# A DiT layer in float32: DeltaNet heads cut into five pieces among the next heads' projections, query latents ahead of the latents of keys and values

## The chip, the cores and the metric

The kernel runs on one core of one Trainium2 chip. The metric is the device time of one execution in microseconds (us). In the profile PE is the tensor engine's matmuls and PEld its weight loads, DVE the vector engine, ACT the scalar engine, POOL the GpSimd engine and SP the engine whose queue issues all DMAs. Each engine works through its own queue in the order in which the program left it, and waits there for the results that an operation needs.

## The reference

One layer of a hybrid diffusion backbone: 256 latent tokens and 256 context tokens of width 2048, all float32. Cut to what matters here:

```
h = modulate(rmsnorm(x), shift, scale)              # latent and context tokens
q_a, kv_a, k_rope, dq, dk, dv, dz, gates... = split(h @ w_in)
# latent attention (8 heads)
k, v = mla_kv(kv_a, k_rope, ...)                    # rmsnorm(kv_a) @ w_kv_b, head norm, rotary
q    = mla_q(q_a, ...)                              # rmsnorm(q_a) @ w_q_b, head norm, rotary
y_mla = attend_latent(q, k, v, context keys and values)
# gated DeltaNet (8 heads, chunks of 64, two directions)
k = l2norm(silu(conv3(dk))); v = silu(conv3(dv)); q = l2norm(silu(conv3(dq))) * 128**-0.5
m   = strict_lower(beta * (k k^T) * decay)          # one 64 x 64 matrix per chunk, head, direction
sol = triangular_solve(I + m, rhs)                  # the kernel inverts I + m
scan over the chunks with sol, k * decay, q * decay, (q k^T) * decay
# then gates, output projections, and a gated MLP with a depthwise convolution
```

## The kernel before

A float32 product is made of two or three products of rounded parts: a weight tile is loaded in halves of 128 x 1024 (`raw`, four buffers), and each 512 columns are split by ACT (`whi`, the rounded copy) and DVE (`wlo`, the rest), six buffers of each. `mm_hl` then issues a pair of matmuls for each 128 rows of the contraction: `whi` against 512 columns (both parts of the activations), `wlo` against 256. The activations are `H[0]` (latent tokens; `h_92` in the order of instructions) and `H[1]` (context tokens; `h_93`). A projection (`proj`) of 128 output columns runs over 16 such rows for one or both token sets (`segs`), so it takes 16 or 32 pairs.

The part that the change touches comes after the first norm. For each DeltaNet head, `head_inputs` projects keys (`wdk`) and values (`wdv`) for both token sets and queries (`wdq`) for the latent tokens; for the heads 0, 1 and 2 keys and values exist already (`dkx`). `dn_head` then does the head's own work: `dn_unit` is the convolution (DVE, tile `cy`), a tanh on ACT (`ct`), the squares (`sqk`), their column sums on PE (`sp`), the scale (`l2m`: DVE, then a power on POOL), two diagonal tiles (`rb_d`, DVE), which a pair of matmuls spreads over all partitions (`bp`), and the scaled result `KT` or `QT`, with its mirrored copy for the backward direction from ACT. The K products `kk` give `U`, which goes to memory in six DMAs (`Ud`, `Uo`); `qk` gives `A`; the values' tile is `VT`; K and V are turned by eight PE transposes each (`tp`) into `KE` and stored. The heads come in the order 0, 3, 1, 4, 2, 5, 6, 7. Beside all this `ada`, a generator, adds up the rest of the modulation vector on DVE (`acc`, one 128 x 512 tile `rawa` of weights per unit, 256 units in all); here it gets a budget of 4,000 (`ADB`) per head, at 650 a unit.

After the heads, `inverse` loads all `U` (`ux<-Ud`), runs 60 dependent operations on DVE (`ux<-ux`), copies the result (`xt`, ACT) and stores it in 32 small DMAs (`Xd`, `Xs`). It is given `IK` of budget after each of the four projections of the latents of keys and values (`wkva`, tile `kvx`), and `IQ` after each of the four of the query latents (`wqa`, tile `qax`). The norms of both (`bk`, `bq`), the split latents `kvn` and `qan_`, and the rotary key (`krf`, which is copied by a DMA to the other half of the partitions and then split to `krt`) follow. `fill` is a generator of gate projections (tile `gtp`, weights `wz`, then `wgm`), 16 pairs a tile, that is drawn on as filler. The attention then begins with the keys (`kps`), their norm (`ksq`, `ks`) and the values (`vps`), beside the first off-diagonal products of the inversion (`ivp`, with tiles `xd` loaded from `Xd`).

A scheduler takes the program in the order in which it is written as priority, and settles from that and its own model the fixed order of each engine's queue.

Of the kernel before, what the change touches and what calls it, by code (L numbers as in the profile page):

```python
# [25 lines left out]
N1 = 3  # L26
# [15 lines left out]
OD = 8000  # L42
OC = 4000
WO = 900
IK = 5000
IQ = 4000
NW = 3
R0 = 1.3
R1 = 1.0
# [4 lines left out]
@with_exitstack  # L54
def hybrid_block(ctx: ExitStack, tc: tile.TileContext, io, dbg=None):
    nc = tc.nc
    act, dve, pool, pe, sync = nc.scalar, nc.vector, nc.gpsimd, nc.tensor, nc.sync


    def pool_(name, bufs, side="left"):  # L60
# [90 lines left out]

        pool.tensor_tensor(out=out, in0=in_, in1=half.broadcast_to([P, n]), op=ALU.pow)

    def row_bcast(pl, ps, r, n):
# [6 lines left out]
        for k, v in enumerate((rh, rl)):  # L161
            dg = pl.tile([P, n, P], F32R, tag="rb_d", name="rb_d", bufs=2)
            dve.tensor_tensor(out=dg, in0=idb, in1=v.unsqueeze(2).broadcast_to([P, n, P]), op=ALU.mult)
            pe.matmul(ps[:, : n * P], onesr, dg.rearrange("p a b -> p (a b)"), start=k == 0, stop=k == 1)
# [234 lines left out]
    pB = ctx.enter_context(ExitStack())  # L399
    pb = pB.enter_context(pool_("pb", 1))  # L400

    def proj(src, segs):
        W = load_w(src)
        pss = [psm.tile([P, 512], F32, tag="mm", name="mmp") for _ in segs]
        for k in range(KD):
            for ps, s in zip(pss, segs):
                mm_hl(ps, P, W(k * P), H[s][:, k], k == 0, k == KD - 1)
        return pss


# [114 lines left out]
        act.activation(t, y, AF.Tanh)  # L525
        return y, t

    def dn_unit(x, f, ns, post, dst):
# [3 lines left out]
        sq = pb.tile([P, 2, T], F32, tag="ct", name="sqk")[:, :ns]  # L532
        act.activation(sq, y, AF.Square)
        n = 2 * ns
# [5 lines left out]
        dve.tensor_scalar(out=m, in0=sp[:, :n], scalar1=post, scalar2=EPS * post, op0=ALU.mult, op1=ALU.add)  # L540
        rsq(pb, m, m, n)
        bp = psa.tile([P, 512], F32, tag="aux", name="bp")
        row_bcast(pb2, bp, m, n)
        for s in range(ns):
            dve.tensor_tensor(out=dst[:, 4 * s : 4 * s + 4, 0], in0=bp[:, s * T : (s + 1) * T].rearrange("p (s i) -> p s i", i=64),
                              in1=y[:, s].rearrange("p (s i) -> p s i", i=64), op=ALU.mult)
        reverse(dst, ns)
# [4 lines left out]
            act.copy(v[:, :, 1], v[:, ::-1, 0, ::-1])  # L552

    def dn_head(h, kx, vx, qx):
        KT = pb2.tile([P, 8, 2, 64], F32, tag="KT", name="KT")
        dn_unit(kx, 8 + h, 2, 1.0, KT)
        sync.dma_start(KTs[:, :, h].rearrange("s p c -> p s c"), KT.rearrange("p s d i -> p s (d i)"))
        QT = pb2.tile([P, 4, 2, 64], F32, tag="QT", name="QT")
        dn_unit(qx, h, 1, 128.0, QT)
# [21 lines left out]
        y, t = dn_conv(vx, 16 + h, 2)  # L581
        VT = pb2.tile([P, 8, 2, 64], F32, tag="KT", name="VT")
        dve.scalar_tensor_tensor(out=VT[:, :, 0], in0=t.rearrange("p a (s i) -> p (a s) i", i=64), scalar=1.0,
                                 in1=y.rearrange("p a (s i) -> p (a s) i", i=64), op0=ALU.add, op1=ALU.mult)
        reverse(VT, 2)
        for which, src, scr in (("k", KT, KEs), ("v", VT, Vs)):
            o = pb2.tile([P, 8, P], F32, tag="KE", name="KE")
            for q in range(2):
                tp = psa.tile([P, 4, P], F32, tag="aux", name="tp")
                for j in range(4):  # L590
                    pe.transpose(tp[:, j], src[:, 4 * q + j].rearrange("p d i -> p (d i)"), ident)
                if which == "k":
                    dve.tensor_tensor(out=o[:, 4 * q : 4 * q + 4], in0=tp,
                                      in1=kb[:, 4 * q : 4 * q + 4, h].unsqueeze(2).broadcast_to([P, 4, P]), op=ALU.mult)
                else:
                    act.copy(o[:, 4 * q : 4 * q + 4], tp)
            sync.dma_start(scr[:, :, h].rearrange("s p c -> p s c"), o)

    def head_inputs(h):
        if h < N1:  # L600
            xs = [dkx[:, 2 * h], dkx[:, 2 * h + 1]]
        else:
            xs = []
            for w in ("wdk", "wdv"):
                pss = proj(io[w][h], (0, 1))
# [138 lines left out]
    kvx = pn.tile([P, 4, 2, T], F32, name="kvx")
    for f in range(4):
        pss = proj(io["wkva"][f], (0, 1))
        for s in range(2):
            gather(pss[s], P, kvx[:, f, s])
        inv(IK)
    bk = pn.tile([P, 2, T], F32, name="bk")  # L750
    rms_bcast(pn2, 4, lambda k: (kvx[:, k, 0], kvx[:, k, 1]), 1.0 / 512, bk)
    qax = pn.tile([P, 4, T], F32, name="qax")
    for f in range(4):
        gather(proj(io["wqa"][f], (0,))[0], P, qax[:, f])
        if f == 2:
            for k in range(4):
                dve.scalar_tensor_tensor(out=kvx[:, k], in0=kvx[:, k], scalar=kvan[:, k : k + 1], in1=bk, op0=ALU.mult, op1=ALU.mult)
                split(kvx[:, k], kvn[:, k, 0], kvn[:, k, 1])
        inv(IQ)
# [22 lines left out]
    dve.tensor_tensor(out=krf[0:64, 0], in0=krf[0:64, 0], in1=rt[0:64], op=ALU.add)  # L782
    sync.dma_start(krf[64:128], krf[0:64])
# [591 lines left out]
```

## Time and profile before

| | us |
|---|---|
| median of 3 runs | 1940.28 (1939.37 to 1945.17) |
| profiled execution | 1937.21 |
| its span on the core | 1935.4 |
| PE busy | 1826.2 |
| DVE busy | 1437.0 |
| ACT busy | 915.9 |

A row of the profile's groups names line, engine, operation, the tile written and the tiles read, and the count. "Idle before" is the time that the engine stood still just ahead of such an operation, with what ended it. A row of the timeline gives start, duration, and in brackets the wait ahead of it. PE's granted clock is 1.00 at full speed, so that busy time at a lower clock holds less work.

### The profile page before, as it was taken

How to read it: one execution, taken by the hardware profiler on the slowest of the kernel's cores; microseconds unless marked ns; L12 is line 12 of the kernel's file. 1: busy time of each engine (PE TensorE's matmuls, PEld its weight loads, DVE VectorE, ACT ScalarE, POOL GpSimd, SP SyncE). 2: the span in 40 equal slices, each digit the busy share in tenths (PEclk: the TensorE clock that was granted, in tenths of full speed). 3: DMA queues.
4: the chain of work that ended last, by engine and by line, in shares of the span. 5: the costliest groups of instructions: out<-in, count | busy, mean ns of one | idle time of the engine just before them, and what ended most of it. 6: DMA issues, size and time to landing. Idle time of an engine off the chain costs nothing.

```text
span 1935.4 us, 34978 instructions
## 1 busy us (share of the span) xinstructions
PE 1826.2 (94%) x13186; PEld 1552.7 (80%) x13186; DVE 1437.0 (74%) x2854; ACT 915.9 (47%) x1882; POOL 41.7 (2%) x45
## 2 busy tenths in 40 slices
PE   7889988999879999999999997999999999999999
PEld 5677867788678878778888885888888888888887
DVE  4998887777768778656679888887778777755554
ACT  3224443333367656543245545555554555544443
POOL 0000000000000000000000000000000000000000
PEclk7899988999889999999999998999999999999999
DMA  8984576665676777788776886776667565566664
GB/s 319 317 290 163 170 202 204 202 195 183 124 239 209 221 223 227 239 254 260 227 266 206 259 282 201 251 252 184 189 203 236 186 184 186 179 195 200 194 193 128
DMA packets 222521, 418.26 MB, mean 216 GB/s; under 512 B 71504, under 2 KB 113616, under 8 KB 219920
## 3 DMA queue, kind: packets, MB, share of 16 engines
q1 hardware_dynamic: 222352, 416.04, 69.1%
q8 instruction: 103, 1.69, 0.4%
q14 instruction: 66, 0.54, 0.1%
HBM read 387.00 MB, written 28.84 MB: 215 GB/s over the span
## 4 chain that ended last, share of the span: by engine, by line
PE 50%; issue 10%; DMA 6%; DVE 4%; ACT 1%; POOL 0%; SPq 0%; POOLq 0%; DVEq 0%; ACTq 0%
PE fps L141 13%; PE dps L141 8%; PE fps L142 7%; DMA rawa<-in_wada 5%; PE gtp L141 5%; PE dps L142 4%; PE gtp L142 2%; DVE acc L240 1%; DVE wlo L101 1%; PE brp L141 1%; PE kp L1084 1%; PE fps L139 1%; PE yp L1093 1%; DMA raw<-in_wgate 1%; PE op L1105 1%
## 5 line engine op out<-in xcount | busy, mean ns | idle before, releaser
L101 DVE TENSOR_TENSOR wlo<-raw,whi 128x512 fp32r<-128x512 f32 (+1 forms) x940 | 634.9, 685 | 197.4 <-ACT whi L100 186.2
L100 ACT CAST whi<-raw 128x512 fp32r<-128x512 f32 (+1 forms) x940 | 571.7, 618 | 415.5 <-PE dps L141 117.4
L141 PE MATMUL fps<-H,whi 128*128 128x512 f32 x1290 | 461.9, 399 | 5.8 <-DVE H L101 5.8
L142 PE MATMUL fps<-H,wlo 128*128 128x256 f32 x1290 | 363.7, 282 | 2.4 <-DVE wlo L101 2.4
L141 PEld LDWEIGHTS fps<-H,whi 128*128 128x128 f32 x1290 | 243.3, 189 | 62.3 <-DVE H L101 4.8
L142 PEld LDWEIGHTS fps<-H,wlo 128*128 128x128 f32 x1290 | 244.8, 190 | 7.7 <-DVE wlo L101 4.0
L240 DVE SCALAR_TENSOR_TENSOR acc<-rawa,sc,acc 128x512 f32<-128x512 f32 x240 | 179.2, 747 | 76.7 <-DMA rawa<-in_wada 75.4
L141 PE MATMUL mmp<-h,whi 128*128 128x512 f32 x600 | 225.2, 413 | 0.9 <-ACT whi L100 0.9
L141 PE MATMUL gtp<-h,whi 128*128 128x512 f32 x600 | 220.8, 404 | 0.0
L141 PE MATMUL dps<-GB,whi 128*128 128x512 f32 x544 | 193.0, 397 | 0.0
L142 PE MATMUL mmp<-h,wlo 128*128 128x256 f32 x600 | 174.8, 292 | 7.7 <-DVE wlo L101 7.7
L142 PE MATMUL gtp<-h,wlo 128*128 128x256 f32 x600 | 171.0, 285 | 0.0
L142 PE MATMUL dps<-GB,wlo 128*128 128x256 f32 x544 | 153.1, 282 | 0.0
L141 PEld LDWEIGHTS mmp<-h,whi 128*128 128x128 f32 x600 | 117.5, 196 | 27.7 <-ACT whi L100 1.3
L141 PEld LDWEIGHTS gtp<-h,whi 128*128 128x128 f32 x600 | 113.6, 189 | 25.8 <-issue 1.5
L142 PEld LDWEIGHTS mmp<-h,wlo 128*128 128x128 f32 x600 | 118.1, 197 | 10.2 <-DVE wlo L101 8.4
L141 PEld LDWEIGHTS dps<-GB,whi 128*128 128x128 f32 x544 | 102.1, 188 | 25.3
L142 PEld LDWEIGHTS gtp<-h,wlo 128*128 128x128 f32 x600 | 114.2, 190 | 4.2 <-issue 1.0
L142 PEld LDWEIGHTS dps<-GB,wlo 128*128 128x128 f32 x544 | 102.5, 188 | 0.0
L344 PE MATMUL fp<-h,gh 128*128 128x256 f32 (+1 forms) x224 | 60.9, 306 | 17.0 <-ACT h L335 17.0
L319 DVE CUSTOM_DVE_ANT_0 junk<-wt,scb 128x2048 bf16<-128x2048 f32 x32 | 73.1, 2284 | 0.1
L345 PE MATMUL fp<-h,gh 128*128 128x256 f32 (+1 forms) x224 | 65.9, 302 | 1.6 <-DVE h L336 1.4
(599 smaller groups left out, 2960.5 us busy)
## 6 DMA issues: line engine op xcount, KB each, us to landing
rawa<-in_wada SPq DMA_DIRECT2D x256, 256.0 KB, 4.0
raw<-in_wgate SPq DMA_DIRECT2D x82, 512.0 KB, 4.5
raw<-in_wval SPq DMA_DIRECT2D x82, 512.0 KB, 4.4
raw<-in_wdown SPq DMA_DIRECT2D x80, 512.0 KB, 4.3
wt<-in_wadas SPq DMA_DIRECT2D x16, 1024.0 KB, 7.4
raw<-in_wadab SPq DMA_DIRECT2D x32, 512.0 KB, 6.4
raw<-in_wgm SPq DMA_DIRECT2D x32, 512.0 KB, 4.7
raw<-in_wgd SPq DMA_DIRECT2D x32, 512.0 KB, 5.2
```

Of the source, the lines that this page charges most:

```text
L100: act.copy(hi, raw)
L101: dve.tensor_tensor(out=lo, in0=raw, in1=hi, op=ALU.subtract)
L139: pe.matmul(ps[:M, :], hi, xf, start=False, stop=True)
L141: pe.matmul(ps[:M, :], hi, xf, start=first, stop=False)
L142: pe.matmul(ps[:M, :T], lo, x[:, 0, :], start=False, stop=last)
L240: dve.scalar_tensor_tensor(out=acc, in0=w, scalar=c, in1=acc, op0=ALU.mult, op1=ALU.add)
L319: dve.tensor_tensor_reduce(out=junk, in0=w, in1=scb[:, s], scale=1.0, scalar=0.0, op0=ALU.mult, op1=ALU.add, accum_out=m[:, s : s + 1])
L344: pe.matmul(ps, hi, H[s][:, k, 0], start=k == 0 and s == 0, stop=False)
L345: pe.matmul(ps, hi, H[s][:, k, 1], start=False, stop=False)
L1084: pe.matmul(kp[hs, j], kt[:, h, hs], S[:, h, d], start=True, stop=True)
L1093: pe.matmul(yp[:, j], tt[:, 4 * q + j], rs[q][:, j], start=True, stop=True)
L1105: pe.matmul(op[q][:, j, d], S[:, h, d], qe[:, h, 64 * d : 64 * d + 64], start=False, stop=d == 1)
```

## The change

`dn_head` becomes a generator of five pieces: convolutions of V, K and Q; sums of K's squares and the turning of V; scaling of K and sums of Q's squares; scaling of Q, `kk` with `U`, and the turning of K; `qk` with `A` and the scaled Q. Between them it yields costs of 6000, 3800, 3800 and 3400. `proj` calls a function `side` after each of its 16 rows, which draws on the pieces of two heads (of one at the end) and on `ada` in proportion to the projection time issued. The stages are: heads 3 and 0 beside the projections of 4 and 1; 4 and 1 beside 5 and 2; 5 and 2 beside 6; 6 beside 7; and 7 beside the four query-latent projections, whose result lies in the freed tile `dkx`. In these stages PE's operations are kept in the order of the program. After them come the query norm, `qan_` and the rotary key, then the latents of keys and values beside the inversion with a budget of 7000 after each, and two draws on `fill` of 5200 instead of one. The buffers of the squares are separate for K and Q (`sqk`, `sqq`).

```
-IK = 5000
-IQ = 4000
+IK = 7000
...
+        def matmul(self, *a, **k):
+            i = nc.tensor.matmul(*a, **k)
+            if self.pinned:
+                tc.keep_in_program_order(i)
+            return i
...
-    def proj(src, segs):
+    def proj(src, segs, side=lambda c: None):
...
                 mm_hl(ps, P, W(k * P), H[s][:, k], k == 0, k == KD - 1)
+            side(353 * len(segs))
...
     def dn_head(h, kx, vx, qx):
+        y, t = dn_conv(vx, 16 + h, 2)
...
+        ky, ksq = dn_silu(kx, 8 + h, 2, "sqk")
+        qy, qsq = dn_silu(qx, h, 1, "sqq")
+        yield 6000
+        dgs = dn_norm(ksq, 2, 1.0)
+        turn(h, VT, "v", Vs)
+        yield 3800
...
+        dn_scale(ky, dgs, 2, KT)
...
+        dgs = dn_norm(qsq, 1, 128.0)
+        yield 3800
...
+        dn_scale(qy, dgs, 1, QT)
         kk = psa.tile([P, 8, 64], F32, tag="aux", name="kk")
...
+        turn(h, KT, "k", KEs)
+        yield 3400
...
-    order = (0, 3, 1, 4, 2, 5, 6, 7)
-    ins = {h: head_inputs(h) for h in order[:2]}
-    for h in order:
-        dn_head(h, *(ins[h] if h in ins else head_inputs(h)))
-        ada(ADB)
+    ins = {h: head_inputs(h) for h in (3, 0)}
...
+    pe.pinned = True
+    for heads, nxt in (((3, 0), (4, 1)), ((4, 1), (5, 2)), ((5, 2), (6,)), ((6,), (7,)), ((7,), ())):
+        main = sum(5650 if h < N1 else 28200 for h in nxt) or 22600
+        work = Side(chains(*heads))
+        def side(c):
+            work(c * 17000 * len(heads) / main)
+            ada(c * ADB / 22600)
+        for h in nxt:
+            ins[h] = head_inputs(h, side)
+        if not nxt:
+            for f in range(4):
+                gather(proj(io["wqa"][f], (0,), side)[0], P, qax[:, f])
+        work.finish()
+    pe.pinned = False
```

How this moves PE's rows in a head: the norm of head 1 before, from its column sums on (`sp` is the sums, `bp` the spread scale, `mmp` a projection; the second part, after the dots, is the end of its Q norm with `kk`, `qk` and the turning of K).

```order
L148 MATMUL sp<-ones,sqk 32x1 x16
L141 MATMUL mmp<-h_92,whi 128x512
L142 MATMUL mmp<-h_92,wlo 128x256
L142 MATMUL mmp<-h_93,wlo 128x256
L141 MATMUL mmp<-h_92,whi 128x512
L164 MATMUL bp<-rb_d,onesr 128x512 x2
L148 MATMUL sp<-ones,sqk 32x1 x8
...
L164 MATMUL bp<-rb_d,onesr 128x256
L563 MATMUL kk<-KT 64x64 x3
L164 MATMUL bp<-rb_d,onesr 128x256
L563 MATMUL kk<-KT 64x64 x13
```

The same steps of head 3, the first, in the new order:

```order
L63 MATMUL sp<-ones,sqk 32x1 x16
L69 MATMUL tp<-ident,VT 128x128 x8
L63 MATMUL mmp<-h_92,whi 128x512
L63 MATMUL mmp<-h_92,wlo 128x256
...
L63 MATMUL bp<-rb_d,onesr 128x512 x2
L63 MATMUL sp<-ones,sqk 32x1 x8
...
L63 MATMUL bp<-rb_d,onesr 128x256 x2
L63 MATMUL kk<-KT 64x64 x16
L69 MATMUL tp<-ident,KT 128x128 x8
L63 MATMUL mmp<-h_92,whi 128x512
L63 MATMUL mmp<-h_92,wlo 128x256
```

Before, the rows of projections between sp and the first bp number 12, 16, 4, 15, 4, 12, 17 and 13 for the eight heads in their order; now 20, 22, 20, 22, 16, 16, 36 and 28, with the eight transposes of V besides. From the first bp to the second they now number 24, 22, 24, 22, 16, 16, 32 and 30, and from qk to the next head's sp 32 to 60; before, the next head's sp stood 0 to 5 rows behind the turning of V for the third and the fifth head. DVE's rows from the scaled Q of head 3 to the squares' input of head 0 (`cy<-ct,cy` of K), in the new order:

```order
L615 SCALAR_TENSOR_TENSOR U<-kk,E 128x512
L642 TENSOR_TENSOR KE<-tp,kb 128x512 x2
L594 SCALAR_TENSOR_TENSOR VT<-ct,cy 128x8x64
L549 TENSOR_SCALAR cy<-dkx,conv 128x512
L549 TENSOR_SCALAR cy<-cq,conv 128x256
L550 SCALAR_TENSOR_TENSOR cy<-dkx,conv,cy 128x2x255
L550 SCALAR_TENSOR_TENSOR cy<-cq,conv,cy 128x255
L629 TENSOR_TENSOR A<-qk,E 128x256
L631 TENSOR_TENSOR QT<-QT,EG 128x512
L551 SCALAR_TENSOR_TENSOR cy<-dkx,conv,cy 128x2x255
L118 TENSOR_TENSOR wlo<-raw,whi 128x512
L559 SCALAR_TENSOR_TENSOR cy<-ct,cy 128x512
```

SP's queue around the inversion's stores before (`Xd`, `Xs` are the stores, 32 in all, of which the first and the last rows stand here):

```order
L106 DMA raw<-in_wqa 128x1024 x2
L106 DMA raw<-in_wz 128x1024 x2
L106 DMA raw<-in_wkvb 128x1024
L106 DMA raw<-in_wz 128x1024 x3
L652 DMA Xd<-xt 32x32x32
...
L660 DMA Xs<-ux 32x16x32 x2
L714 DMA Zs<-zt 128x256
L783 DMA krf<-krf 64x512
L677 DMA xd<-Xd 128x2x128
L106 DMA raw<-in_wkvb 128x1024
L106 DMA raw<-in_wz 128x1024
```

And now:

```order
L705 DMA ux<-Ud 128x2048
L123 DMA raw<-in_wkva 128x1024 x2
L254 DMA rawa<-in_wada 128x512 x2
L836 DMA krf<-krf 64x512
...
L123 DMA raw<-in_wkvb 128x1024
L782 DMA Zs<-zt 128x256 x2
L123 DMA raw<-in_wz 128x1024
L720 DMA Xd<-xt 32x32x32
...
L728 DMA Xs<-ux 32x16x32 x2
L745 DMA xd<-Xd 128x2x128
L782 DMA Zs<-zt 128x256
L123 DMA raw<-in_wz 128x1024
```

The stores stand as one block in both; krf moved from behind it to ahead of it, and so did the second tile of `wkvb`, with eight loads of `wz` ahead of the block instead of five. In PE's queue 68 pairs of gtp now stand between the last `kvx` projection and the first ivp.

More of the change, by code (lines that the diff above doesn't have):

```diff
@@ L56, in hybrid_block, with transpose @@
     nc = tc.nc
-    act, dve, pool, pe, sync = nc.scalar, nc.vector, nc.gpsimd, nc.tensor, nc.sync
+    act, dve, pool, sync = nc.scalar, nc.vector, nc.gpsimd, nc.sync
+    class TensorE:
+        pinned = False
+        def matmul(self, *a, **k):
[3 more added lines that the diff above has]
+            return i
+        def transpose(self, *a, **k):
+            i = nc.tensor.transpose(*a, **k)
+            if self.pinned:
+                tc.keep_in_program_order(i)
+            return i
+    pe = TensorE()
     def pool_(name, bufs, side="left"):
@@ L526, in dn_conv, with dn_silu, dn_norm @@
         return y, t
-    def dn_unit(x, f, ns, post, dst):
+    def dn_silu(x, f, ns, tag):
         y, t = dn_conv(x, f, ns)
         dve.scalar_tensor_tensor(out=y, in0=t, scalar=1.0, in1=y, op0=ALU.add, op1=ALU.mult)
-        sq = pb.tile([P, 2, T], F32, tag="ct", name="sqk")[:, :ns]
+        sq = pb.tile([P, ns, T], F32, tag=tag, name="sqk")
         act.activation(sq, y, AF.Square)
+        return y, sq
+    def dn_norm(sq, ns, post):
         n = 2 * ns
@@ L580, in dn_head, with turn, head_inputs @@
         sync.dma_start(QEs[:, :, h].rearrange("s p c -> p s c"), QT.rearrange("p s d i -> p s (d i)"))
[L581 to L599, printed above, removed]
+    def turn(h, src, which, scr):
+        o = pb2.tile([P, 8, P], F32, tag="KE", name="KE")
+        for q in range(2):
+            tp = psa.tile([P, 4, P], F32, tag="aux", name="tp")
+            for j in range(4):
+                pe.transpose(tp[:, j], src[:, 4 * q + j].rearrange("p d i -> p (d i)"), ident)
+            if which == "k":
+                dve.tensor_tensor(out=o[:, 4 * q : 4 * q + 4], in0=tp,
+                                  in1=kb[:, 4 * q : 4 * q + 4, h].unsqueeze(2).broadcast_to([P, 4, P]), op=ALU.mult)
+            else:
+                act.copy(o[:, 4 * q : 4 * q + 4], tp)
+        sync.dma_start(scr[:, :, h].rearrange("s p c -> p s c"), o)
+    def head_inputs(h, side=lambda c: None):
         if h < N1:
@@ L604, in head_inputs @@
             for w in ("wdk", "wdv"):
-                pss = proj(io[w][h], (0, 1))
+                pss = proj(io[w][h], (0, 1), side)
                 x = pb2.tile([P, 2, T], F32, tag="cx", name="cx")
@@ L609, in head_inputs @@
                 xs.append(x)
-        ps = proj(io["wdq"][h], (0,))[0]
+        ps = proj(io["wdq"][h], (0,), side)[0]
         xq = pb2.tile([P, 1, T], F32, tag="cq", name="cq")
@@ L616, in hybrid_block, with chains @@
     ada.done = 0
-    order = (0, 3, 1, 4, 2, 5, 6, 7)
-    ins = {h: head_inputs(h) for h in order[:2]}
-    for h in order:
-        dn_head(h, *(ins[h] if h in ins else head_inputs(h)))
-        ada(ADB)
+    ins = {h: head_inputs(h) for h in (3, 0)}
+    def chains(*hs):
+        for h in hs:
+            yield from dn_head(h, *ins.pop(h))
+    qax = dkx[:, 0:2].rearrange("p f s t -> p (f s) t")
+    pe.pinned = True
[12 more added lines that the diff above has]
+    pe.pinned = False
     for nm, t_ in (("KTs", KTs), ("KEs", KEs), ("Vs", Vs), ("QEs", QEs), ("As", As)):
         dump(nm, t_)
-    pX.close()
     pB.close()
@@ L743, in hybrid_block @@
     inv(1)
[L744 to L759, printed above, removed]
     bq = pn.tile([P, 1, T], F32, name="bq")
     rms_bcast(pn2, 4, lambda k: (qax[:, k],), 1.0 / 512, bq)
-    fill(5200)
+    for k in range(4):
+        dve.scalar_tensor_tensor(out=qax[:, k], in0=qax[:, k], scalar=qan[:, k : k + 1], in1=bq[:, 0], op0=ALU.mult, op1=ALU.mult)
+        split(qax[:, k], qan_[:, k, 0], qan_[:, k, 1])
     cosT, sinT, perm = rope["cos"], rope["sin"], rope["perm"]
@@ L784, in hybrid_block @@
     split(krf.rearrange("p a b -> p (a b)"), krt[:, 0], krt[:, 1])
+    kvx = pn.tile([P, 4, 2, T], F32, name="kvx")
+    for f in range(4):
+        pss = proj(io["wkva"][f], (0, 1))
+        for s in range(2):
+            gather(pss[s], P, kvx[:, f, s])
+        inv(IK)
+    fill(5200)
+    bk = pn.tile([P, 2, T], F32, name="bk")
+    rms_bcast(pn2, 4, lambda k: (kvx[:, k, 0], kvx[:, k, 1]), 1.0 / 512, bk)
+    fill(5200)
     for k in range(4):
-        dve.scalar_tensor_tensor(out=qax[:, k], in0=qax[:, k], scalar=qan[:, k : k + 1], in1=bq[:, 0], op0=ALU.mult, op1=ALU.mult)
-        split(qax[:, k], qan_[:, k, 0], qan_[:, k, 1])
+        dve.scalar_tensor_tensor(out=kvx[:, k], in0=kvx[:, k], scalar=kvan[:, k : k + 1], in1=bk, op0=ALU.mult, op1=ALU.mult)
+        split(kvx[:, k], kvn[:, k, 0], kvn[:, k, 1])
     inv.finish()
+    pX.close()
     pH.close()
```

21 lines of the change are left out of this document (16 added, 5 removed).

## The prediction

> **What bounds the kernel now.** I read the page first, then the time by stretches, then the waits inside the stretches that the diff touches, then the rows of single steps. The columns of a stretch are its length, the busy time (and count) of PE, PEld, DVE, ACT and POOL, PE's granted clock, and the DMA share.
>
> ```profile
> span 1935.4 us, 34978 instructions
> PE 1826.2 (94%) x13186; PEld 1552.7 (80%) x13186; DVE 1437.0 (74%) x2854; ACT 915.9 (47%) x1882; POOL 41.7 (2%) x45
> PE   7889988999879999999999997999999999999999
> DVE  4998887777768778656679888887778777755554
> 168.00:215.00 47.00, 46.57 (x249) 36.48 (x248) 40.45 (x86) 24.24 (x50) 0.00 (x0) 1.00 0.40 123
> 215.00:431.00 216.00, 196.30 (x1749) 162.29 (x1749) 172.67 (x361) 84.77 (x175) 16.07 (x16) 0.93 0.70 204
> 431.00:516.00 85.00, 75.71 (x631) 63.48 (x629) 68.38 (x144) 35.55 (x73) 3.14 (x4) 0.90 0.56 160
> 516.00:552.00 36.00, 24.92 (x189) 21.54 (x188) 17.04 (x40) 12.43 (x27) 2.34 (x2) 0.81 0.83 182
> ```
>
> PE is busy in 94% of the span and nearly solid after the first third, so the kernel's time is PE's work plus what PE loses. PE work at full clock is about busy time times clock; the rest of a stretch is loss. 168 to 215 (first projections, gate tables) loses 0.4 us, 215 to 431 (the eight DeltaNet heads) 216 - 196.3 x 0.93 = 33.4, 431 to 516 (latents of keys and values, then of queries) 85 - 75.7 x 0.90 = 16.9, and 516 to 552 (the way into the attention) 36 - 24.9 x 0.81 = 15.8. The change adds and removes no operation: each engine's list is the same but for its order. So the forecast is the profiled execution's 1937.2 us (the median of the three runs, 1940.28, lies 0.16% above) plus the change in these losses. About 0.3%, 6 us, is what a measurement of this kernel can tell from no change.
>
> **Where the first loss is.** The same stretch in five, then PE's waits in it, and single steps.
>
> ```profile
> 215.00:250.00 35.00, 32.83 (x347) 26.75 (x347) 30.01 (x69) 15.70 (x34) 3.76 (x4) 1.00 0.67 193
> 250.00:311.00 61.00, 48.24 (x449) 38.12 (x448) 50.23 (x111) 23.29 (x49) 6.17 (x6) 0.78 0.71 196
> 311.00:375.00 64.00, 62.86 (x508) 53.71 (x508) 49.67 (x93) 25.12 (x52) 2.02 (x2) 1.00 0.75 226
> 375.00:391.00 16.00, 12.88 (x107) 10.56 (x106) 10.33 (x23) 4.08 (x10) 1.96 (x2) 0.89 0.63 179
> 391.00:431.00 40.00, 39.50 (x344) 33.14 (x343) 32.43 (x67) 16.59 (x34) 2.17 (x3) 1.00 0.67 200
> PE bp L164 <- DVE rb_d L163: 10.2, 9, 3.1
> PE sp L148 <- ACT sqk L533: 6.0, 2, 3.3
> 216.99 0.15 DVE L540 TENSOR_SCALAR l2m<-sp 128x4 f32<-128x4 f32 x1
> 219.69 0.68 DVE L163 TENSOR_TENSOR rb_d<-ident,rb_l 128x512 fp32r<-128x512 f32 x1
> 301.48 0.61 PE L148 MATMUL sp<-ones,sqk 128*32 128x1 f32 x32 [2.78 <-ACT sqk L533]
> 303.56 0.63 PE L141 MATMUL mmp<-h,whi 128*128 128x512 f32 x1
> 271.46 0.28 PE L142 MATMUL mmp<-h,wlo 128*128 128x256 f32 x1
> 271.58 0.39 PE L141 MATMUL mmp<-h,whi 128*128 128x512 f32 x1
> 271.81 0.28 PE L142 MATMUL mmp<-h,wlo 128*128 128x256 f32 x1
> 379.22 0.75 DVE L240 SCALAR_TENSOR_TENSOR acc<-rawa,sc,acc 128x512 f32<-128x512 f32 x1 [3.02 <-DMA rawa<-in_wada]
> 383.08 0.80 PE L164 MATMUL bp<-rb_d,onesr 128*128 128x512 f32 x1 [3.12 <-DVE rb_d L163]
> ```
>
> A head's norm is a chain over engines: column sums on PE (sp), l2m on DVE, a power on POOL, two diagonal tiles on DVE (rb_d), PE again (bp). From l2m at 216.99 to the diagonals' end at 220.4 it takes 3.4 us, twice per head. PE waits for it, or for the squares ahead of sp. The loss lies in one place: 250 to 311 loses 61 - 48.2 x 0.78 = 23.4 us. There heads follow each other with 0 to 5 rows of projections between turning and sp or sp and bp (the order in the section on the change). 375 to 391 loses 4.5, where DVE waited 3.0 us for a rawa load and bp 3.1 us for DVE. The other three stretches, 139 us with four heads, lose 2.2 + 1.1 + 0.5 = 3.8 us, 0.95 per head; there 12 to 16 rows lie between sp and bp. 13.7 us of the 33.4 are clock (196.3 x 0.07): behind the wait of 2.78 us the 512-column matmul takes 0.63 us instead of 0.39. A pair, hi and lo, takes 271.81 - 271.46 = 0.35 us at full clock.
>
> **The change, part 1: heads in pieces.** Between sp and bp PE now meets 16 to 36 rows of projections (8 to 18 pairs, 2.8 to 6.3 us) and V's turn, between the first bp and the second 16 to 32, and from qk to the next sp 32 to 60. That is as much as in the three good stretches or more, in every head. So I carry over their 0.95 us: 8 x 0.95 = 7.6 us. Waits for rawa remain (5.0 us of acc's idle time in the row below): one more stop like that at 383, 4.5 with its clock.
>
> DVE is the tighter side. The stage now also holds the query latents, 64 pairs: PE work 182.6 + 64 x 0.35 = 205 us. DVE had 172.7 busy; the latents add 16 splits of 0.69 and four additions, 13 us: 186, or 90% of PE's time, where the good stretches had 86, 78 and 81%. For that I add 2 us. Loss 14 instead of 33.4, a gain of 19.4. Bounds: 6 if DVE is always in time; 33 if the waits only change place.
>
> ```profile
> L101 DVE TENSOR_TENSOR wlo<-raw,whi 128x512 fp32r<-128x512 f32 x61 | 41.1, 686 | 8.6 <-ACT whi L100 7.5 <-DMA rawa<-in_wada 0.3
> L240 DVE SCALAR_TENSOR_TENSOR acc<-rawa,sc,acc 128x512 f32<-128x512 f32 x40 | 29.8, 746 | 5.1 <-DMA rawa<-in_wada 5.0
> ```
>
> The products of the modulation (acc) are spread over the projections; their budget in the stage falls from 32,000 to 26,000, nine units. Nine loads of 256 KB and nine times 0.75 us of DVE move to the last stages, where PE's row reads 9 and DVE's 5 to 8: no cost. SP's stores of a head are the same, spread too. Loads of weights queue behind stores that wait for DVE, with four buffers ahead; I count that inside the 2.
>
> **Part 2: queries ahead of keys and values.** The inversion of the heads' matrices, which needs every head's U, now meets other work:
>
> ```profile
> 437.76 1.18 SPq L637 DMA_DIRECT2D ux<-Ud  x1
> ux<-Ud SPq DMA_DIRECT2D x1, 1024.0 KB, 7.4
> 446.35 0.21 DVE L642 TENSOR_TENSOR ux<-ux 128x60 f32<-128x60 f32 x1
> 505.93 0.27 DVE L644 TENSOR_TENSOR ux<-ux 128x60 f32<-128x60 f32 x1
> 507.16 2.13 ACT L649 COPY xt<-ux 128x1024 f32<-128x1024 f32 x1
> 509.32 0.33 SPq L652 DMA_DIRECT2D Xd<-xt  x1
> 532.89 1.13 SPq L660 DMA_DIRECT2D Xs<-ux  x2
> 534.60 0.54 SPq L783 DMA_DIRECT2D krf<-krf  x1
> 536.92 0.62 ACT L100 CAST krt<-krf 128x512 fp32r<-128x512 f32 x1 [0.20 <-DMA krf<-krf]
> 541.52 0.61 PE L148 MATMUL ks<-ones,ksq 128*32 128x1 f32 x32 [11.08 <-ACT ksq L827]
> raw<-in_wz SPq DMA_DIRECT2D x10, 512.0 KB, 4.9
> ```
>
> 60 us of DVE (446.4 to 506.2, other operations between), 3.1 to the end of xt, then 32 stores that fill SP's queue from 509.3 to 534.1, 24.8 us in which no weight is asked for. Behind them stood krf, and behind krf's split on ACT the keys' evictions: PE idle for 11.1 us. The change issues krf ahead of the stores, so that wait goes. Late next: 68 pairs of wz (gtp) stand ahead of the first off-diagonal product (ivp), and the last four use a weight tile loaded behind the stores. With the end of the query latents as 0: ux issued at 5 (A and QE of the last head, two stores, one load, rope), landed at 12.4, inversion over at 72, xt at 75.5, stores at 100.3, the weight tile issued 1.4 later, landed after 4.9 and split, so PE goes on at 107. PE's work up to there: keys and values 128 pairs (45), norms and rope 1.5, 64 pairs of gtp (22.6), 24 products each of keys (0.24) and values (0.12), 8.5, sums 1.1: 79 us. Loss 28, plus 2 for DVE waiting on krf's load (behind two weight loads in SP's queue), plus 4 of slow clock: 34, against 16.9 + 15.8 = 32.7 now. The wait for krf gives way to one for the stores themselves, since 22.6 us of query latents no longer lie beside the inversion and only one more wz tile (5.6 us) comes in. So this part is worth -1.3 us. Bounds: 24 if the inversion takes 10 us less, since wqa's 16 splits no longer stand among its operations; 44 if it takes 10 more, with all norms in the same queue.
>
> Sum: 1937.2 - 19.4 + 1.3 = 1919.1.
>
> The Trainium skill ("TensorE: Matmul & The Clock Gate", Part 1, the HAM clock gate) says that the gate opens after about 3.4 us of sustained work and closes after an idle window of the same length. Here it closed after a wait of 2.78 us, so the trace disagrees on the closing. By the page's figures a long stop would cost 1.7 us of clock (half of 3.4) instead of my 4, an estimate that would give about 1917.
>
> **The rivals.** (1) The inversion is covered better. For it: only half of its present 32 splits stand in its 60 us. Part 2 then loses 20 instead of 34, and the time is 1905. (2) No change: DVE, at 90% and in order, is late for most chains, and PE, held to program order, has nothing else to do. For it: at 383 PE waited although 12 rows stood there, because DVE was late. Against it: the three good stretches. The loss stays at 33 and the time is 1938. (3) Slower: the next head's three convolutions (7 us of DVE, with turns through ACT) end later than PE's 11 us from the second bp to sp, in every head, and PE waits the whole delay at low clock. It decides from 33.4 / 8 = 4.2 us per head; at 6 the stage loses 48 and the time is 1953. Against it: in the printed order DVE has some 9 us of operations in these 11.
>
> **How the numbers follow.** Forecast (1919, own range 1908 to 1931) 0.56; rival 1 (1905) 0.17; rival 2 (1938) 0.19; rival 3 (1953) 0.08. Faster by over 0.3% (under 1934.5): the first two but for 0.01, and a quarter of rival 2, 0.77. Slower (over 1946): rival 3 but for 0.01, 0.07. Same: 0.16. The range 1901 to 1940 leaves out rival 3 and a tail of rival 1.
>
> **What would show it.** Right: idle time before bp and sp under 10 us in all, and a clock of 0.97 or more over the heads, which with the query latents last about 220 us; krf issued ahead of the 32 stores; a PE wait of over 10 us beside those, ended by a wz load or by ivp. Wrong: waits at bp as long as now (then DVE, not PE's order, sets them), or no long wait beside the stores. Most likely to make it wrong is the DVE order, which a scheduler laid out with its own durations.

## The result, and the profile after

The changed kernel takes 1920.68 us (median of six runs, 1918.22 to 1929.33) against 1940.88 for the kernel before (six runs). The recorded ratio is 0.9908, interval 0.9891 to 0.9924; the two medians alone divide to 0.9896. So it is 18 to 20 us faster, and the time is the forecast's (1919.1). The parts of the sum did not come out as written: the heads gained more than forecast, stretches that the sum left out lost time, and the two errors cancel.

The profiled execution of the changed kernel took 1929.33 us, the slowest of the six. From its page:

```profile
span 1927.4 us, 35016 instructions
PE 1818.1 (94%) x13186; PEld 1548.1 (80%) x13186; DVE 1429.2 (74%) x2854; ACT 914.4 (47%) x1882; POOL 44.1 (2%) x45
PE   7888999999599998999999996989999999999999
PEclk7899999999799999899999997999999999999999
```

Each engine's count of instructions in that row is the one before. PE's row, which showed 8 and 9 in turn over the heads, is solid there now; one slice further right reads 5. Two stretches by time for each kernel, the changed one first. They begin and end at the same amount of PE work (busy time times clock, summed from the span's start), so that a row of one can be set beside a row of the other:

```profile
180.00:408.00 228.00, 227.06 (x1985) 189.14 (x1984) 199.96 (x422) 111.00 (x228) 18.38 (x16) 1.00 0.72 209
408.00:535.00 127.00, 102.51 (x870) 86.54 (x869) 92.49 (x200) 51.67 (x110) 5.61 (x6) 0.91 0.65 174
```

```profile
180.00:438.00 258.00, 237.94 (x1997) 194.71 (x1996) 207.41 (x427) 104.91 (x214) 16.07 (x16) 0.94 0.65 189
438.00:567.00 129.00, 108.63 (x846) 92.63 (x845) 94.56 (x201) 57.20 (x124) 5.49 (x6) 0.88 0.65 174
```

The heads took 258 us and take 228. PE is busy in all of it, at full clock. The second stretch, the latents and the way into the attention, takes 127 instead of 129. So the gain lies in the first, and up to 535 us the changed kernel is 32 us ahead. At the end it is only 8 ahead, in this execution, which is the slowest of the six: 24 us were given back where nothing was forecast. By the medians it would be some 12 to 14.

To see where, I took windows of 5 us over the whole span (loss is 5 minus busy time times clock) and summed them between marks of equal PE work: 133, 360, 460, 760, 1020 and 1160 us of work. In the changed kernel these are the times 180, 408, 535, 865, 1130 and 1300. Finer windows give somewhat smaller losses than the prediction's long ones (28 instead of 33 us for the latents before), since a long stretch's mean clock also counts slow clock under idle time. All kernels of this study, in us of lost PE time:

| kernel (time of the profiled execution's span) | start | heads | latents | attention to scan | scan, outputs | into feed-forward | rest |
|---|---|---|---|---|---|---|---|
| before (1935.4) | 47.3 | 31.2 | 28.4 | 15.1 | 5.0 | 19.7 | 5.9 |
| changed (1927.4) | 46.9 | 0.9 | 27.4 | 29.4 | 5.2 | 30.5 | 4.8 |
| e1_unpinned (1914.2) | 51.5 | 0.7 | 27.6 | 18.9 | 5.8 | 25.9 | 4.2 |
| e2_heads_alone (1908.6) | 47.4 | 1.6 | 25.2 | 12.9 | 7.6 | 27.1 | 4.7 |
| e3_latents_alone (1937.1) | 54.6 | 28.4 | 19.2 | 15.7 | 6.6 | 20.1 | 4.3 |
| e4_two_zt (1917.1) | 51.1 | 0.5 | 27.9 | 22.0 | 5.2 | 24.8 | 5.5 |
| e5_ada_budget (1920.8) | 54.3 | 2.0 | 31.1 | 18.9 | 8.5 | 21.2 | 5.6 |
| e6_one_fill (1909.5) | 48.3 | 0.7 | 26.8 | 14.9 | 6.4 | 26.2 | 5.1 |
| e7_one_store (1922.9) | 48.6 | 0.5 | 13.5 | 45.1 | 6.9 | 24.6 | 4.5 |
| e8_heads_one_store (1921.1) | 51.9 | 1.9 | 10.0 | 36.7 | 10.3 | 26.0 | 5.5 |
| e9_zeros_early (1910.4) | 51.6 | 0.3 | 25.0 | 18.6 | 6.5 | 24.2 | 4.7 |
| e10_copies_on_pool (1893.5) | 49.4 | 0.3 | 13.5 | 11.4 | 6.8 | 26.3 | 6.2 |
| e11_no_fill (1917.3) | 51.6 | 0.7 | 28.1 | 19.9 | 6.6 | 24.9 | 4.2 |
| e12_heads_pool (1895.0) | 50.9 | 1.1 | 10.0 | 13.5 | 10.4 | 22.8 | 4.4 |

Each row is one execution, and the clock has two decimals. The changed kernel and e1, whose programs are nearly the same, differ by 4.6 us in the start and by 10.5 from the attention to the scan, so that a difference of a few us in one column shows little by itself. A row's sum is its span less the PE work counted in it, 1779 to 1788 us. Where the query latents stay behind (before, e2, e8, e12), the same marks hold a little of the key latents in the second column.

The waits of PE that answer to the prediction's, first in the changed kernel's heads (180 to 408, us in total, times, longest), then in its latents:

```profile
PE bp L63 <- DVE rb_d L181: 0.2, 1, 0.2
```

```profile
PE ks L63 <- ACT ksq L891: 20.3, 1, 20.3
```

The 16.2 us at bp and sp are gone. The 11 us at ks, ended by the keys' squares, have become 20 at the same place. The timeline of ScalarE, SyncE's queue and PE there (start, duration, and in brackets the idle time before the instruction and what ended it):

```profile
427.17 0.55 SPq L836 DMA_DIRECT2D krf<-krf  x1
486.70 0.32 SPq L720 DMA_DIRECT2D Xd<-xt  x1
...
509.67 1.53 SPq L728 DMA_DIRECT2D Xs<-ux  x2
511.30 0.44 SPq L745 DMA_DIRECT2D xd<-Xd  x1
511.78 0.47 SPq L782 DMA_DIRECT2D Zs<-zt  x1
491.28 0.42 ACT L779 ACTIVATE zt<-zx 128x256 f32<-128x256 f32 x1 [0.43 <-DVE zx L408]
495.61 1.08 ACT L117 CAST kt<-kps 128x512 fp32r<-128x512 f32 x2
514.55 0.42 ACT L779 ACTIVATE zt<-zx 128x256 f32<-128x256 f32 x1 [17.86 <-DMA Zs<-zt]
514.88 0.58 ACT L891 ACTIVATE ksq<-kps 128x512 f32<-128x512 f32 x1
515.51 0.61 PE L63 MATMUL ks<-ones,ksq 128*32 128x1 f32 x32 [20.26 <-ACT ksq L891]
```

Read from below: PE's column sums wait for the squares (ksq). The squares stand on ScalarE behind the next gate tile's tanh (zt). That has one buffer, whose last content (491.28) is still to be stored, and its store (511.78) stands in SyncE's queue behind the 32 stores of the inversion, 486.7 to 511.2. krf went out at 427, long ahead. The kernel before shows the same chain just ahead of the row for krf's split that the prediction gives (536.92):

```profile
536.31 0.42 ACT L711 ACTIVATE zt<-zx 128x256 f32<-128x256 f32 x1 [8.27 <-DMA Zs<-zt]
```

ScalarE stood 8.27 us there for zt's store, and then only 0.20 us for krf. Both had been issued right behind the block of stores (534.12 and 534.60), so moving krf alone could not take the wait away. The block of stores stops PE before and after the change, through whatever stands behind it.

### The profile page after: what moved, and what is told of

It reads as the page before. It is cut to its first block, busy times and chain, and to the rows that moved or that the text cites. A ratio compares the mean times of both kernels' runs of the same rounds, so it can differ in the third digit from the quotient of the medians.

```text
span 1927.4 us, 35016 instructions
## 1 busy us (share of the span) xinstructions
PE 1818.1 (94%) x13186; PEld 1548.1 (80%) x13186; DVE 1429.2 (74%) x2854; ACT 914.4 (47%) x1882; POOL 44.1 (2%) x45
## 4 chain that ended last, share of the span: by engine, by line
PE 50%; issue 10%; DMA 7%; DVE 4%; ACT 1%; POOL 0%; SPq 0%; POOLq 0%; DVEq 0%; ACTq 0%
PE fps L63 21%; PE dps L63 13%; PE gtp L63 7%; DMA rawa<-in_wada 6%; PE brp L63 2%; DVE wlo L118 1%; DVE acc L267 1%; PE op L63 1%; PE vps L63 1%; PE yp L63 1%; PE kp L63 1%; DMA raw<-in_womla 1%; DMA raw<-in_wgate 1%; PE ivp L63 1%; PE yps L63 1%
## 5 line engine op out<-in xcount | busy, mean ns | idle before, releaser
L63 PE MATMUL fps<-H,whi 128*128 128x512 f32 x1376 | 484.0, 399 | 5.4 <-DVE H L118 5.4
L63 PE MATMUL fps<-H,wlo 128*128 128x256 f32 x1376 | 375.2, 282 | 6.1 <-DVE wlo L118 6.1
L63 PEld LDWEIGHTS fps<-H,whi 128*128 128x128 f32 x1376 | 254.5, 189 | 61.7 <-DVE H L118 3.3
L63 PEld LDWEIGHTS fps<-H,wlo 128*128 128x128 f32 x1376 | 261.2, 190 | 16.7 <-DVE wlo L118 9.1
L63 PE MATMUL gtp<-h,whi 128*128 128x512 f32 x640 | 235.1, 403 | 0.1
L63 PE MATMUL dps<-GB,whi 128*128 128x512 f32 x560 | 199.2, 397 | 0.0
L63 PEld LDWEIGHTS gtp<-h,whi 128*128 128x128 f32 x640 | 120.7, 189 | 26.2 <-issue 1.5
L63 PEld LDWEIGHTS gtp<-h,wlo 128*128 128x128 f32 x640 | 121.5, 190 | 5.7 <-issue 0.9
L63 PE MATMUL fp<-h,gh 128*128 128x256 f32 (+1 forms) x448 | 93.2, 305 | 18.2 <-ACT h L362 16.5
L63 PEld LDWEIGHTS fp<-h,gh 128*128 128x128 f32 (+1 forms) x448 | 75.0, 203 | 30.1 <-ACT h L362 20.5
```

The source lines that it names most:

```text
L63: i = nc.tensor.matmul(*a, **k)
```

## The experiments

Ratios are to the kernel before, timed beside it on the same chip.

**e1_unpinned**

```diff
-    pe.pinned = True
+    pe.pinned = False
```

> The changed kernel without TensorE's program order over the heads; pieces and places stay. The scheduler's own order then differs from the pinned one at four places only. Theory (the written places of the pieces make the gain): no wait of over 2 us at bp or sp, the heads lose under 3 us of TensorE, 1921 within 4. Rival (the pin makes it): waits at bp return, some 20 us of the stage's 31 come back, 1938.

Measured: 1917.97, ratio 0.9915 (0.988 to 0.995), as the changed kernel's 0.9908. The heads lose 0.7 us; the wait at bp is the same 0.2. So without the pin the scheduler's own order does as well: the gain comes from the written places of the pieces, not from the pin.

**e2_heads_alone and e3_latents_alone.** The first is the changed kernel with `wqa` and the latents in their old order; beside the last head nothing is written. The second is the kernel before with the changed kernel's latents (queries first, krf ahead of the keys, two draws of gate tiles).

```diff
 e2, against the changed kernel          e3, against the kernel before
-  if not nxt: proj(wqa) beside head 7   +  proj(wqa) behind the last head
+  wkva, norm, wqa, norm, fill, krf      -  wkva, norm, wqa, norm, fill, krf
-  norm, krf, wkva, fill, norm, fill     +  norm, krf, wkva, fill, norm, fill
```

> Part 1 alone: heads in pieces, but keys' and values' latents ahead of the queries' as before; the last head has no projection beside it. Theory (the pieces take nearly all of the 33 us that the heads lost, and part 2 is worth about nothing): the heads lose 2 us, the uncovered last head some 5, the latents 33 as before, so 1915 to 1922, and the wait behind krf's load stays at about 11 us. Rival (my account on record, 14 us still lost in the heads): 1926 or more.

> Part 2 alone: heads whole and in the scheduler's order as before, query latents ahead of keys and values. Theory: the heads lose 33 us as before, krf's wait of 11 us goes, a stop of 10 to 20 us beside the 32 stores takes its place, 1940 within 5. Rival (part 2 carries a good share of the gain): 1930 or less.

Measured: part 1 alone 1911.46, ratio 0.9877 (0.9847 to 0.9908); part 2 alone 1935.10, 0.9991 (0.9969 to 1.0014). PE's waits in the latents of the first, then of the second from 160 to 415 us (most of the heads) and in its latents:

```profile
PE ks L64 <- ACT ksq L895: 13.6, 1, 13.6
PE mmp L64 <- DVE wlo L119: 4.4, 1, 4.4
```

```profile
PE bp L163 <- DVE rb_d L162: 8.6, 8, 2.3
PE sp L147 <- ACT sqk L532: 6.3, 2, 3.2
PE ks L147 <- ACT ksq L824: 13.3, 1, 13.3
```

The pieces carry the whole gain, and the rest of the change adds nothing to them; the medians even lie 0.3% the other way, at the intervals' edges, and part 1 alone is below its forecast (1915 to 1922). The part called pieces also holds the separate buffers of the squares and the smaller budget of ada. The budget is not what wins: with more of those products e5 still loses only 2.0 us in the heads. The buffers were not tested alone. The last head without projections written beside it cost 1 us, not 5. The wait at ks is 13.6 us with krf behind the stores (e2) and 13.3 with krf ahead of them (e3), as is to be expected if krf's place is worth nothing. In e3's profiled execution the latents lose 9 us less than before and the start 7 more; over its ten runs nothing is left of the nine that the interval would show.

**e4_two_zt**

```diff
-        x = pz.tile([P, T], F32, tag="zx", name="zx")
-        t = pz.tile([P, T], F32, tag="zt", name="zt", bufs=1)
+        x = pz.tile([P, T], F32, tag="zx", name="zx", bufs=1)
+        t = pz.tile([P, T], F32, tag="zt", name="zt", bufs=2)
```

> The changed kernel with two buffers for zt (and one for zx, which pays the space); TensorE's order is the same to the row. Theory (the keys' squares stood on ScalarE behind a tanh that waited for zt's only buffer, whose store stood in SyncE's queue behind the 32 stores): the wait of 20.3 us at ks goes, TensorE runs on to the first off-diagonal product and waits there for its load, which stands behind the same stores, 10 to 14 us; 1914 (1911 to 1918). Rival (the squares wait for something else behind the stores, such as a weight tile): a wait of 18 us or more at ks stays, 1921.

Measured: 1920.03, ratio 0.9937 (0.9903 to 0.9971): nothing won. PE's waits there, and a row of VectorE:

```profile
PE vps L63 <- DVE km L900: 9.4, 1, 9.4
PE ks L63 <- ACT ksq L891: 3.4, 1, 3.4
PE gtp L63 <- ACT whi L117: 2.7, 1, 2.7
516.15 0.16 DVE L900 SCALAR_TENSOR_TENSOR km<-ks,krm 128x4 f32<-128x4 f32 x1 [13.22 <-DMA Xs<-ux]
```

The wait at ks fell from 20.3 to 3.4, so the chain through zt is right. But the keys' mean (km) then waited for the last store of ux itself, and gtp for a weight tile asked for behind the stores. I take the first for a reuse of ux's space; the row shows only that the store released it. The latents lose 27.9 instead of 27.4. The expectation named the first off-diagonal product as the next stop, and its gain of 6 us did not come: three different things stand behind the same block, and taking one away moves the stop to the next.

**e5_ada_budget**

```diff
-ADB = 4000
+ADB = 5000
```

> The changed kernel with the modulation's budget beside the heads raised from 4000 to 5000, so that about as many of its products run there as before the change (47 instead of 35 to 37). Theory (the 12 products that moved to later stages cost time there): the heads lose at most 3 us more, the stretch from the output projections to the first third of the feed-forward loses 5 less and the way into the scan some 3 less; 4 to 6 us below the changed kernel (which should run about 1918 here), 1913. Rival (they are free in the late stages, and VectorE beside the heads is at its limit): 5 to 10 us more in the heads and nothing back, 1923 or more.

Measured: 1925.49, ratio 0.9950 (0.9930 to 0.9969). Products (acc) beside the heads and on the way into the feed-forward (the number behind x; first and last start), with the larger budget, then in e1_unpinned, then on that way in the kernel before:

```profile
L267 DVE SCALAR_TENSOR_TENSOR acc<-rawa,sc,acc x40: 740/748/755, 188.7 to 413.9; 128x512 f32<-128x512 f32 x40
L267 DVE SCALAR_TENSOR_TENSOR acc<-rawa,sc,acc x47: 741/748/754, 1146.4 to 1295.4; 128x512 f32<-128x512 f32 x47
```

```profile
L267 DVE SCALAR_TENSOR_TENSOR acc<-rawa,sc,acc x35: 737/748/753, 186.2 to 411.5; 128x512 f32<-128x512 f32 x35
L267 DVE SCALAR_TENSOR_TENSOR acc<-rawa,sc,acc x44: 740/748/754, 1138.1 to 1275.1; 128x512 f32<-128x512 f32 x44
```

```profile
L240 DVE SCALAR_TENSOR_TENSOR acc<-rawa,sc,acc x37: 739/750/753, 1156.8 to 1282.3; 128x512 f32<-128x512 f32 x37
```

The edit did not do what it was made for: five more products ran beside the heads, not twelve, and none fewer on the way into the feed-forward. So it settles nothing on what the moved products cost. The heads lost 1 us more, so VectorE had room there. Yet the kernel is slower than the changed one by 0.4%, with intervals that do not meet, and its time is the rival's (1923 or more). In the profile the latents lose 31.1 instead of 27.4; what made them is open.

**e6_one_fill and e11_no_fill.** The changed kernel draws gate tiles twice around the norm of keys and values, the kernel before once. e6 drops the first draw, e11 both. (A gate tile is 16 pairs, so 32 products; the 64 in the expectation is a slip, its 5.6 us are right.)

```diff
         inv(IK)
-    fill(5200)
     bk = pn.tile([P, 2, T], F32, name="bk")
     rms_bcast(pn2, 4, lambda k: (kvx[:, k, 0], kvx[:, k, 1]), 1.0 / 512, bk)
     fill(5200)
```

> The changed kernel without the first of its two draws of 5200 from the gate tiles around the norm of keys and values: one gate tile (64 products, 5.6 us) stays for later, as before the change. Theory (that tile is what is missing ahead of the scan, where TensorE waited 3.3 us for the scan's load and ran at half clock): the latents lose some 5 us more, the stretch from the attention to the scan 8 less; 1916. Rival (that wait has another cause, the loads of the moved products): the stretch loses as much as now, 1923.

> e6_one_fill without the second draw from the gate tiles either. Theory (the end of the stop is set by the stores, not by the work ahead of it, and each gate tile kept is worth its 5.6 us later): the stop 5 us longer, the attention and the scan's start 5 to 8 less, 1911 within 4. Rival (the later stretches have cover enough with one tile back): the stop's 5 us are lost, 1917.

Measured: e6 1911.67, ratio 0.9871 (0.9848 to 0.9894); e11 1918.05, 0.9907 (0.9875 to 0.9939). PE's waits on the way into the scan, in the changed kernel and then in e6:

```profile
PE yp L63 <- DMA jit<-Xs: 3.3, 1, 3.3
PE rps L63 <- ACT qx L927: 2.7, 1, 2.7
```

```profile
PE yps L63 <- DVE PT L118: 1.8, 1, 1.8
PE rps L63 <- ACT qx L926: 1.6, 1, 1.6
```

With one draw less the scan's load is not waited for, and the stretch from the attention to the scan loses 14.9 instead of 18.9 (e1) to 29.4. A wait of 1.7 to 5.4 us for one of the scan's loads shows in five kernels with two draws (changed, e1, e3, e4, e7; not in e5), and in none of the others, which draw once or not at all. By the ratios (0.9871 against 0.9908) the extra tile cost some 7 us; their intervals just touch, and e9, also with one draw, loses 18.6 in that stretch. Its removal cost the latents nothing, against my 5. That fits a stop whose end is set elsewhere. But the reason I gave, that a tile kept back is worth its 5.6 us, does not hold: e11 keeps another one and loses 5 us more in that stretch than e6. Its time is the rival's (1917), though not by the stop, which lost 1 us more and not 5.

**e7_one_store and e8_heads_one_store.** The inversion's result goes to a DRAM copy (Xr) in one DMA; the 16 strided pieces follow from there beside the attention, two by two with the off-diagonal products, and the zeros come early from the identity's corner. e7 is the changed kernel so edited, e8 is e2.

```diff
-            ... Xs[bs, bs] <- X[hs, b]          # 4 per g, in the block
-            ... Xs[32:64, h, 0:32] <- tmp[0:32] # 2 per g, in the block
+        sync.dma_start(Xr, flat)
...
+            if q % 2:
+                spread_x(q // 2)                # Xs[bs, bs] <- Xr, zeros <- ident
```

> The changed kernel with the inversion's result stored by nine DMAs instead of 32: the eight Xd stores and one of the whole tile to a copy in DRAM; the 16 strided ones go later from that copy, beside the attention, and the eight stores of zeros go early, from a constant. Theory (everything in that stop waits for the 24.8 us that the stores fill in SyncE's queue): the wait of 18 to 20 us at ks and its followers fall to 6 us in all, the latents' stretch loses 10 instead of 27.5, 1902 (1897 to 1908). Rival (the stop only changes place once more, or the later copies hold up weights): 1912 or more.

> The same nine stores in the kernel with part 1 alone, where the latents keep their old order. Theory: the wait of 13.6 us at ks goes there too, the latents' stretch loses 10 instead of 25 us, 1897 (1892 to 1903), and part 2 stays worth nothing or less without the block of stores. Rival: without the block the query latents' place counts, and e7_one_store is the faster of the two.

Measured: e7 1933.01, ratio 0.9980 (0.9964 to 0.9996); e8 1918.90, 0.9922 (0.9899 to 0.9946). e7 is slower than the changed kernel that it was made from, and e8's median lies above e2's, with intervals that overlap a little. PE's waits of e7 in the latents, then in the attention; below, SyncE's queue and PE in e8's attention:

```profile
PE ks L63 <- ACT ksq L899: 6.7, 1, 6.7
PE gtp L63 <- ACT whi L117: 13.6, 3, 7.7
PE qps L63 <- ACT whi L117: 6.7, 1, 6.7
```

```profile
538.30 0.33 SPq L124 DMA_DIRECT2D raw<-in_wz  x1
...
556.08 1.21 SPq L732 DMA_DIRECT2D Xs<-Xr  x2
563.40 2.04 SPq L774 DMA_DIRECT2D Xs<-uo  x4
565.54 1.61 SPq L790 DMA_DIRECT2D Zs<-zt  x1
567.20 0.93 SPq L255 DMA_DIRECT2D rawa<-in_wada  x2
568.17 0.90 SPq L124 DMA_DIRECT2D raw<-in_wgm  x2
574.76 0.80 PE L64 MATMUL gtp<-h,whi 128*128 128x512 f32 x1 [6.35 <-ACT whi L118]
```

The first half of the theory held: the latents lose 13.5 us (10 forecast) and 10.0 (10). Then the attention loses 45.1 and 36.7, and both times miss their forecasts (1902 and 1897). e7's is in its rival's range; e8's rival, that e7 would be the faster of the two, is wrong as well. From 538.6 to 568.2 the queue asks for no tile of `raw`: copies and stores stand in it, some of which wait for their producers (it is idle from 557.3 to 563.4, ahead of a store of uo), and PE stops at 574.76 for a tile asked for at 568. The four copies in these 30 us hold the queue for only 2.3; the weight loads stand behind all the rest as well.

**e9_zeros_early** (made from e6)

```diff
+        for h in range(HEADS):   # ahead of the inversion; the scheduler sets them into the first heads
+            sync.dma_start(Xs[:, :, 32:64, h, 0:32]..., ident[0:32, 32:64]...)
...
-            for h in (2 * g, 2 * g + 1):
-                sync.dma_start(Xs[:, :, 32:64, h, 0:32]..., tmp[0:32]...)
```

> e6_one_fill, with the eight stores of zeros taken out of the block of 32 and issued long ahead, from a constant; the 24 others stay where they are. Theory (the stop's length is the block's length in SyncE's queue): eight stores of 0.6 to 0.75 us less, the stop and the latents' loss 5.5 us shorter, 1906 where e6_one_fill runs 1912. Rival (the stop's end hangs on something else behind the stores, or the loss only moves on): 1911.

Measured: 1905.16, ratio 0.9857 (0.9824 to 0.9890); the wait at ks:

```profile
PE ks L63 <- ACT ksq L889: 15.6, 1, 15.6
```

18.8 us in e6, 15.6 here. The median is the forecast's (1906), but the latents lose 1.8 us less, not 5.5, and the ratio's interval holds e6's. The traces show why the loss fell so little. From the first store of xt to its end the block takes 23.2 us in e6 (488.25 to 511.44) and 18.8 in e9 (491.00 to 509.81), 4.4 shorter. But the inversion, whose load was issued 1.1 us earlier than in e6, ended 2.7 us later, so that the block's end moved by 1.6 only. The direction fits, the size is not shown.

**e10_copies_on_pool and e12_heads_pool.** e10 is e7 with one draw of gate tiles as in e6, e12 is e8; in both the copies' queue is changed:

```diff
-                sync.dma_start(Xs[:, :, bs, 4 * a + g, bs]..., Xr[...])
+                pool.dma_start(Xs[:, :, bs, 4 * a + g, bs]..., Xr[...])
```

> e6_one_fill with the nine stores of e7_one_store, and the 16 later copies issued by GpSimd's queue instead of SyncE's, so that no weight load stands behind one. Theory (in e7 and e8 the copies in SyncE's queue put weight loads late, and that took the gain back): the latents lose 10 to 13 instead of 27 us and the attention's stretch 15 as in e6_one_fill, 1898 (1893 to 1904). Rival (the loss in the attention comes from the shorter stop itself, an order laid out for other times, or from the copies' own traffic): the attention loses 10 to 20 more again, 1910 or more.

> e10_copies_on_pool with the latents in their old order (part 1 alone, nine stores, the 16 copies from GpSimd's queue). Theory (the place of the query latents is worth nothing either way once no extra gate tile is drawn and the block of stores is gone): the latents lose 10 us as in e8_heads_one_store, the attention 13 to 15, 1894 (1890 to 1899), the same as e10_copies_on_pool within 4. Rival (part 2 pays when the stores no longer cut it short): 1902 or more.

Measured: e10 1895.98, ratio 0.9805 (0.9766 to 0.9844); e12 1900.18, 0.9827 (0.9795 to 0.9859). Waits of e10 in the latents, and its stretch 523 to 665:

```profile
PE ks L63 <- ACT ksq L898: 6.6, 1, 6.6
```

```profile
523.00:665.00 142.00, 140.07 (x1149) 122.16 (x1148) 109.97 (x235) 97.02 (x234) 13.41 (x15) 1.00 0.73 226
```

Now the latents lose 13.5 and 10.0 us and the attention 11.4 and 13.5: the shorter stop is kept. e8 and e12 differ only in the queue that issues 16 copies, and in the order that the scheduler then lays out: 23 us in the attention of the profiled executions, 18 by the ratios. Where e8's queue asks for no tile of `raw` from 538.6 to 568.2, e12's asks for six. e10 also draws once where e7 draws twice, so those two differ by more than the queue. e10 beats both kernels: the one before by 40 us, timed beside it, the changed one by some 20 (0.9805 against 0.9908). And e12, with the latents in their old order, just outside its forecast (1890 to 1899), is the same within the intervals: part 2 is worth nothing that these runs can tell.

## Why the prediction was right and wrong

The total was right by luck: two errors cancelled. By its own steps:

- **Part 1, loss of the heads.** Forecast 14 us, measured 0.9 (0.7 in e1): the term of the sum that was mis-sized, by 13. I carried over 0.95 us per head from the good stretches of before, and added 4.5 for a stop at rawa and 2 for VectorE. None of the three came. VectorE's load was as forecast (199.96 of 228 us, 88%), and it was in time for every chain: the longest wait at bp is 0.2 us. The load says little where the chain's next step stands 16 rows away. Marks that were right: waits under 10 us at bp and sp, a clock of 0.97 or more (1.00). The gain was 30 us (31.2 lost before, by the finer windows), not 19. Rival 2 and rival 3 both expected VectorE late; it was not, by more than 0.2 us.
- **Part 2, size.** Forecast a change of +1.3 us; by the prediction's own formula 127 - 102.51 x 0.91 = 33.7 now against 129 - 108.63 x 0.88 = 33.4, by the finer windows 27.4 against 28.4. Its chain of times, from the end of the query latents at 410, held: ux issued at 5 (measured 5), the inversion over at 72 (74), the stores out at 100.3 (101), PE going on at 107 (105.5). Of the 34 us that it gave the stretch, the waits took 24.4 (30 forecast) and the slow clock 2.9 (4).
- **Part 2, cause.** Wrong step: "The change issues krf ahead of the stores, so that wait goes". The wait at ks was put down to krf, but the row of krf's split has 0.20 us of wait; the 8.27 us ahead of it were zt's, whose only buffer waited for its store behind the block. So the wait stayed, now 20.3 us, and it was ended by the keys' squares, not "by a wz load or by ivp". e4 shows that the name mattered little: with that path open, km and the weight tile waited for the same stores. The block of stores was the term: with nine stores instead of 32 the stretch loses 13.5 (e7, e10) and 10.0 (e8, e12).
- **The clock after the stop.** I took 4 us of slow clock. PE's rows after the stop:

```profile
520.67 0.63 PE L63 MATMUL vps<-whi,kvn 128*128 128x256 f32 x2
521.30 0.40 PE L63 MATMUL vps<-whi,kvn 128*128 128x256 f32 x2
```

  Two products take 0.63 us until 521.3 and 0.40 from there: 5.8 us at half speed from 515.5, a loss of 2.9. (After the stop at 383 in the kernel before, full speed came back 3.2 us after the work began.) The Trainium skill ("TensorE: Matmul & The Clock Gate", Part 1, the HAM clock gate) has the gate open after about 3.4 us of sustained work, from which I had estimated 1.7. The trace lies between that and my 4.
- **What I set to zero.** Nine loads and products that move to the last stages ("no cost"), and one more gate tile that "comes in" as cover beside the stop. The stretches from the attention to the feed-forward lost 25 us more in the profiled execution, 11 in e1's. Of this the extra gate tile is some 7 us by the ratios of e6; the cover bought nothing where it was put, since the stores set the end of that stop. For the rest, the way into the feed-forward loses 20 us in before and in e3, 21 to 31 in every kernel with the pieces, of which e1 runs 44 products there, e2 and e5 47, instead of 37. But e5 lost 21.2 and e2, with as many, 27.1: that the products are the cause is not shown, and it stays open.

So the sum was -30 (not -19.4) for the heads, about 0 (+1.3) for the latents and some +10 (0) behind them. Rival 1 was wrong: the inversion was not covered better. A time like its 1905 came only with edits beyond the change, without the extra draw and the block of stores (e10: 0.9805 x 1940.88 = 1903).

## What to carry to other kernels

Cut a chain that goes over several engines into pieces and write each beside enough of the next step's independent work; where that was done in the source here, the order did not need the pin, and a consumer 16 rows away or more hid an engine that was 88% busy. Before you put a wait down to one operation, read what its engine waited for just ahead of it. When a stop moves to a new place after its cause was taken away, list everything that stands behind the same block of an in-order queue, and shorten the block or send it by another queue, not the first path that the profile names. Work drawn forward as cover is missing later: count it in both places.

## What the runs showed of the hardware

- SyncE's queue is held by the issue of stores: the 32 take 24.5 us, 0.3 to 0.9 each. The 16 strided ones among them, one megabyte in all, take 14.2; the one DMA that stores the same megabyte in e7 takes 0.9 us of the queue.
- GpSimd's queue issued a strided copy from DRAM to DRAM as quickly as SyncE's: 0.63 us median over 16 in e10, against 0.55 in e7, with 4.8 and 3.0 us to landing (median; the rows give the issue, least, median and longest ns, first and last start):

```profile
L732 POOL DMA_DIRECT2D Xs<-Xr x16: 630/630/801, 500.5 to 552.9; - x16
```

```profile
L732 SPq DMA_DIRECT2D Xs<-Xr x16: 540/549/1662, 507.8 to 657.4; - x16
```

- The first 180 us lose 46.9 to 54.6 us, in one execution of each of these kernels, with next to the same instructions there: a spread of 8 us where no edit was aimed, as large as several of the effects above.
